# A decoder block's down projection in seven block products, ordered together with the up projection

## The chip, the cores and the metric

The kernel computes one layer of a decoder block on one core of a Trainium2 chip. The metric is the device time of one execution in microseconds (us). TensorE (PE) multiplies, VectorE (DVE), ScalarE (ACT) and GpSimd (POOL) do the rest, and SyncE (SP) issues the transfers between HBM and the core's SBUF; matmul results stand in PSUM, of which the kernel uses banks of 128x512 f32. All numbers are of type f32 outside; a change of about 0.2% is what a measurement of this kernel tells from no change.

## The reference, cut to what matters

Sequence and model width are both 1024, the inner width of the feed-forward part is 2816 = 22 x 128.

```python
mixed = (jax.nn.sigmoid(gate_a) * (o_a @ w_branch_gdn[i])
         + jax.nn.sigmoid(gate_b) * (o_b @ w_branch_nsa[i]))
h = layer_norm(DN_ALPHA * x + mixed @ w_out[i], ln1_g[i], ln1_b[i])
u = causal_dwconv(h @ w_up[i], ffn_conv_w[i])
u_g, u_v = jnp.split(u, 2, axis=-1)
f = (jax.nn.silu(u_g) * u_v) @ w_down[i]
x = layer_norm(DN_ALPHA * h + f, ln2_g[i], ln2_b[i])
```

o_a is a gated delta rule, o_b a sparse attention with compressed, selected and windowed keys. The change concerns `@ w_down`: a 1024 x 2816 gated product, stored by columns of 128 inner units, times a 2816 x 1024 weight.

## The kernel before, in words

**Precision.** An f32 operand is split into a high part (type fp32r) and a low part (what the rounding left), and each product is made of three matmuls: high by high, high by low, low by high. `mm` (L190, matmul at L191) issues each. A split is an ACT copy (high) and a subtraction (low).

**Stages.** x is transposed and v projected; then the delta rule and the input projections; then key compression; from about 630 to 895 us of the span the attention; then the branch products, W_out and the first layer norm; from about 1127 to 1499 us the up projection; from there to 1750.5 us the down projection; then what is left of the second layer norm.

**Attention.** 16 units, one for each block t of 128 tokens and group g of heads. For a unit PE makes scores for two branches (b = 0, selected keys, and b = 1, window), woven with the products by V of the unit before (`weave`, L980). The probabilities P are scaled by `scale` (L865): three of four heads by POOL (L873), one by ACT. After that PE transposes them by identity matmuls (L946), ACT copies the high part (L948) and DVE subtracts the low part (L949). L938 is POOL's scaling for the compressed keys, L882 the reciprocals' gate factors on DVE. At the end of a unit `fin` uses one buffer of the weight stream (tag `w`, three buffers, one of which holds the masks during the attention). In this stage only the order on PE is written out; the other engines' orders follow from priorities of the tile framework.

**Up projection.** 22 groups f of 128 + 128 output units (gate and value). Each group is a 2x2 block product over token halves and halves of the model width that is made in seven products of 24 or 12 matmuls in place of eight. Its sums go through DVE (`u1`, `u2`, `u3`, `c12`, `c21`, `c22`; L1480 to L1501); ACT and DVE apply the three taps of the convolution (L1382, L1466), ACT the tanh (L1508), and DVE the gating (L1512, L1513), after which the two PSUM banks a and d are free. The gated product of group f, 128 x 1024, lies in `accs` and is stored to `gdr[f]` in HBM (L1515). High weights are split by ACT, low ones by POOL (L1371) in the steady part. All this is ordered by `Plan` (L53): a list scheduler on planned durations, with pools of tokens for buffers (`ring`, `raw`, `bank`, `u`, `acc`) and due times; each engine's list is then issued in the order found.

**Down projection.** Two passes, one per token half; each goes over 22 blocks f. Per block the 512 KB of weight are loaded (`w`), split by ACT (L1564) and POOL (L1565), and the 256 KB half of `gdr[f]` (`tb`), split by ACT (L1572) and DVE (L1573); then 4 token blocks x 2 output halves x 3 matmuls of 128x512. The last KL = 6 blocks of a pass go row block by row block, so that the layer norm of one row block lies under the matmuls of the next: L1607 adds the residual, L1177 to L1187 make mean and scale (`rsqrt` on POOL, L387), L1190 normalises on ACT, L1620 and L1621 apply gain and bias.

Of the kernel before, what the change touches and what calls it, by code (L numbers as in the profile page):

```python
# [22 lines left out]
NFF = 2816 // 128  # L23
MS = {mybir.EngineType.PE}
# [28 lines left out]
class Plan:  # L53
# [16 lines left out]
    def rank(self):  # L70
# [7 lines left out]
        for n in self.nodes:  # L78
            n.late = n.asap if n.seq else (n.due if n.due is not None else n.asap + 6.0)
            n.open = n.seq or n.due is not None  # L80
# [7 lines left out]
    def run(self):  # L88
# [10 lines left out]
        while left:  # L99
# [4 lines left out]
            for e in free:  # L104
                if free[e] > t + 1e-9:
                    continue
                for n in todo[e]:
# [14 lines left out]
                    for p, tokens in n.grow:  # L122
                        back += [(n.end, p, x) for x in tokens]
# [21 lines left out]
def hybrid_block_kernel(ctx: ExitStack, tc: tile.TileContext, x, w_in, gdn_conv_w, gdn_a_log,  # L145
# [274 lines left out]
    gA = S6.tile([128, 4, T], F32, name="gA", tag="s")  # L420
    sig = [dram.tile([128, T], F32, name=f"sig{j}") for j in range(16)]
# [568 lines left out]

    prev = None
# [136 lines left out]
    gdr = [dram.tile([128, T], F32, name=f"gdr{f}") for f in range(NFF)]  # L1128
# [71 lines left out]
    P.pool("acc", 0)  # L1200
# [133 lines left out]
    def wide(_):  # L1334
# [7 lines left out]
          [stored[t] for t in range(4, 8)] + [turned[t] for t in range(4, 8)], lat=0, grow=[("acc", [0, 1])])  # L1342
# [15 lines left out]
    def make(f, n, src, deps, give=()):  # L1358

        fast = {"G": 1.25, "V": .65} if f < 3 else "G"  # L1360
# [33 lines left out]

    class Group:
        def __init__(self, f):
            self.f, self.n, self.t = f, {}, {}

        def weights(self, part):
            f = self.f  # L1400
            if part == 0:
# [5 lines left out]
                if 0 < f < AHEAD:  # L1407
                    last.give.append((w1, "raw"))
                return
            w1 = load_raw(f * 128, 0) if 0 < f < AHEAD else self.w1  # L1410
            w2 = load_raw((NFF + f) * 128, 0)
            A11, A12 = (lambda: w1.tile[:, HS[0]]), (lambda: w1.tile[:, HS[1]])
            A21, A22 = (lambda: w2.tile[:, HS[0]]), (lambda: w2.tile[:, HS[1]])
            e = {"G": 1.25, "V": .65} if f < 2 else "G"
# [8 lines left out]
            wait = [state[tt]["end"] for tt in range(4, 8)] if f == 0 else []  # L1423
# [29 lines left out]
        def after(self, n):  # L1453
# [3 lines left out]
            acc = lambda i: accs()[:, (f % 2) * 2 + i, :]  # L1457
# [31 lines left out]
            elif n == 4:  # L1489

                N["sa"] = scaled(0, "a", 0, f, [N[2], chain.get("acc", None)], take=["acc"])
# [8 lines left out]
            else:  # L1500
# [6 lines left out]
                for h, bank in enumerate("ad"):  # L1507
# [3 lines left out]
                    def g_(_, h=h, bank=bank):  # L1511
# [3 lines left out]
                N["end"] = P.add("S", 1.5, lambda _: nc.sync.dma_start(gdr[f], acc(0)), out, lat=2.0,  # L1515
                                 give=[(N["sa"], "acc")])
                chain["acc"] = N["sa"]

    groups = [Group(f) for f in range(NFF)]
# [10 lines left out]
    for f, g in enumerate(groups):  # L1530
        for n in ([6, 7, 5, 4, 3] if f < AHEAD else [1, 6, 7, 5, 2, 4, 3]):
            g.run(n)
    order = P.run()
# [7 lines left out]

    hR, l2 = [], []

    def load_rest():
        for th in range(2):
            t = S2a.tile([128, 4, D], F32, name=f"hr{th}", tag="s")
            for i in range(4):
                nc.sync.dma_start(t[:, i, :], hres[th * 4 + i])
            hR.append(t)
        for src in (ln2_g, ln2_b):  # L1550
            for hs in HS:
                t = tile_u()
                nc.sync.dma_start(t, bass.AP(tensor=src.tensor, offset=src.offset + hs.start, ap=[[0, 128], [1, 512]]))
                l2.append(t)

    wd = {}

    def down_load(th, f):
        if f % 2 == 0:
            wd["pair"] = S6.tile([128, 2, 2, D], F32R, name="wd", tag="s")  # L1560
        w = wtile()
        nc.sync.dma_start(w, w_down[f * 128:(f + 1) * 128, :])
        o = wd["pair"][:, f % 2]
        A.activation(o[:, 0], w, AF.Copy)  # L1564
        G.tensor_tensor(o[:, 1], w, o[:, 0].bitcast(F32), op=OP.subtract)  # L1565
        r = tp.tile([128, 512], F32, name="tb", tag="tb")
# [91 lines left out]
```

## Time and profile before

| | |
|---|---|
| median of 3 runs | 1762.13 us (1759.58 to 1763.2) |
| profiled execution | 1762.67 us, of which the span of the instructions is 1761.0 us |
| mean granted TensorE clock | 0.991 of full speed |
| matmuls, attention to the end of up (630 to 895, 1127 to 1499 us) | 1580 and 1622 records |
| down projection | 1056 matmuls |
| DMA over the span | 152.38 MB, 87 GB/s |

A window's row gives its stretch, its length, then for each engine the busy time with the number of records, then the granted clock, the DMA engines' share and the GB/s that they moved. A timeline's row gives start, duration, engine, line, operation, output <- inputs, shape, and in brackets the idle time before it with what ended it. A source's row gives the shortest, median and longest duration in ns. Some records of matmuls can be missing from a trace.

### The profile page before, as it was taken

The numbers are of one execution on the slowest core, as the hardware profiler recorded it, in microseconds if no ns is written. First come the engines' busy times: TensorE is split into PE (matmuls) and PEld (weight loads), VectorE is DVE, ScalarE is ACT, GpSimd is POOL, SyncE is SP. The second block draws the span as 40 slices with busy tenths as digits, with TensorE's granted clock in tenths as the row PEclk, the third lists the DMA queues.
The fourth block names the chain that finished last, engine by engine and source line by source line (L and its number), as shares of the span: only waits on it lengthen the run. The fifth ranks groups of instructions, "written<-read, shape, count | busy, mean of one in ns | idle before, by whom it ended". The sixth has DMA issues, their size and how long they took to land.

```text
span 1761.0 us, 23301 instructions
## 1 busy us (share of the span) xinstructions
PE 1719.1 (98%) x8710; PEld 1440.8 (82%) x8710; DVE 1100.4 (62%) x2068; ACT 732.2 (42%) x1282; POOL 804.8 (46%) x589
## 2 busy tenths in 40 slices
PE   8999999999999999999989999999999999999997
PEld 8888888888888877888768787788888888888886
DVE  3566757667633378899843348976666566844535
ACT  3422323233223468888732225444444444432321
POOL 1332221222213424444466236777777775764631
PEclk9999999999999999999989999999999999999999
DMA  5222121222212200000045512322222222863421
GB/s 173 73 64 72 55 74 43 74 51 61 78 62 73 68 1 1 1 1 1 25 132 191 192 48 96 108 84 84 88 80 74 89 89 96 315 223 110 171 89 48
DMA packets 157807, 152.38 MB, mean 87 GB/s; under 512 B 16329, under 2 KB 129150, under 8 KB 157694
## 3 DMA queue, kind: packets, MB, share of 16 engines
q1 hardware_dynamic: 157693, 150.89, 27.1%
q8 instruction: 69, 1.13, 0.3%
q14 instruction: 45, 0.36, 0.1%
HBM read 119.67 MB, written 31.20 MB: 86 GB/s over the span
## 4 chain that ended last, share of the span: by engine, by line
PE 85%; DVE 6%; issue 3%; ACT 2%; POOL 2%; DMA 1%; DVEq 0%; POOLq 0%; ACTq 0%; SPq 0%
PE pq L191 35%; PE big L191 33%; PE sm L191 13%; PE sm L946 3%; ACT P L911 1%; DVE st L909 1%; DVE wb L1371 1%; DVE accs L1382 0%; DVE wl L949 0%; POOL h L1228 0%; POOL h L1229 0%; DMA w<-in_w_out_dram 0%; PE big L245 0%; DVE gs L1573 0%; DVE oAl L1013 0%
## 5 line engine op out<-in xcount | busy, mean ns | idle before, releaser
L181 POOL TENSOR_TENSOR wl<-w,wh 128x1024 fp32r<-128x1024 f32 (+2 forms) x51 | 122.6, 2408 | 361.8 <-PE big L191 131.2
L191 PE MATMUL big<-xTl,wh 128*128 128x512 f32 x624 | 250.6, 402 | 0.0
L191 PE MATMUL big<-xTh,wh 128*128 128x512 f32 x624 | 250.3, 401 | 0.0
L191 PE MATMUL pq<-wd,gs 128*128 128x512 f32 x1056 | 241.5, 391 | 0.4 <-DVE accs L1513 0.4
L191 PEld LDWEIGHTS pq<-wd,gs 128*128 128x128 f32 x1056 | 198.2, 188 | 43.3 <-DVE accs L1513 0.8
L191 PE MATMUL pq<-xb,wb 128*128 128x512 f32 x792 | 189.0, 393 | 2.6 <-DVE accs L1382 2.1
L1382 DVE SCALAR_TENSOR_TENSOR accs<-pq,fcw,accs 128x510 f32<-128x510 f32 (+3 forms) x264 | 145.8, 569 | 63.3 <-ACT accs L1466 58.1
L191 PEld LDWEIGHTS pq<-xb,wb 128*128 128x128 f32 x792 | 149.7, 189 | 35.6 <-ACT wb L1172 2.5
L191 PE MATMUL big<-xTh,wl 128*128 128x512 f32 x624 | 164.1, 399 | 0.0
L873 POOL TENSOR_TENSOR P<-P,st 128x640 f32<-128x640 f32 (+7 forms) x96 | 99.8, 1067 | 127.0 <-DVE st L882 61.4
L1565 POOL TENSOR_TENSOR wd<-w,wd 128x1024 fp32r<-128x1024 f32 x44 | 112.5, 2575 | 65.3 <-ACT wd L1564 59.8
L191 PEld LDWEIGHTS big<-xTl,wh 128*128 128x128 f32 x624 | 117.7, 189 | 21.3 <-issue 0.2
L191 PEld LDWEIGHTS big<-xTh,wh 128*128 128x128 f32 x624 | 117.7, 189 | 21.1
L191 PEld LDWEIGHTS big<-xTh,wl 128*128 128x128 f32 x624 | 114.0, 188 | 22.0
L191 PE MATMUL pq<-mTh,wb 128*128 128x512 f32 x528 | 127.3, 397 | 3.2 <-ACT mTh L1172 3.1
L191 PE MATMUL pq<-mTl,wb 128*128 128x512 f32 x528 | 127.4, 391 | 0.0
L191 PEld LDWEIGHTS pq<-mTh,wb 128*128 128x128 f32 x528 | 100.8, 191 | 25.7 <-ACT mTh L1172 3.3
L1371 POOL TENSOR_TENSOR wb<-w,wb 128x512 fp32r<-128x512 f32 x79 | 102.8, 1302 | 37.8 <-ACT wb L1172 37.8
L191 PEld LDWEIGHTS pq<-mTl,wb 128*128 128x128 f32 x528 | 99.1, 188 | 21.2
L1573 DVE TENSOR_TENSOR gs<-tb,gs 128x512 fp32r<-128x512 f32 x44 | 71.4, 1641 | 67.0 <-ACT gs L1572 64.2
L949 DVE TENSOR_TENSOR wl<-sm,wh 128x512 fp32r<-128x512 f32 (+1 forms) x148 | 99.8, 684 | 13.7 <-ACT wh L948 11.3
L180 ACT ACTIVATE wh<-w 128x1024 fp32r<-128x1024 f32 (+2 forms) x51 | 53.1, 1046 | 127.1 <-PE big L191 85.9
(365 smaller groups left out, 3543.2 us busy)
## 6 DMA issues: line engine op xcount, KB each, us to landing
w<-in_w_down_dram SPq DMA_DIRECT2D x44, 512.0 KB, 4.1
w<-in_w_in_dram SPq DMA_DIRECT2D x40, 512.0 KB, 4.1
w<-in_w_up_dram SPq DMA_DIRECT2D x36, 512.0 KB, 3.8
gdr<-accs SPq DMA_DIRECT2D x22, 512.0 KB, 2.6
tb<-gdr SPq DMA_DIRECT2D x44, 256.0 KB, 3.2
sig<-th SPq DMA_DIRECT2D x32, 256.0 KB, 2.4
w<-sig SPq DMA_DIRECT2D x16, 512.0 KB, 3.4
wx<-in_w_up_dram SPq DMA_DIRECT2D x11, 512.0 KB, 3.8
```

What stands on the lines that cost most here:

```text
L180: A.activation(wh[:, :n], w[:, :n], AF.Copy)
L181: G.tensor_tensor(wl[:, :n], w[:, :n], wh[:, :n].bitcast(F32), op=OP.subtract)
L191: PE.matmul(o, a, b, start=start, stop=stop, skip_group_check=True)
L873: G.tensor_tensor(p, p, r.to_broadcast([128, p.shape[1]]), op=OP.mult)
L909: V.reduce_max(nm, pv if m > 1 else pv[:, 0], axis=AX.X, negate=True)
L911: A.activation(P[:, r0 + i, :n], pv[:, i], AF.Exp, bias=nm[:, i:i + 1], accum_out=su[:, i:i + 1])
L946: PE.transpose(tp[:n, r * 128:(r + 1) * 128], P[:, r, c0:c0 + n], ident)
L949: V.tensor_tensor(pl, tp[:n], ph.bitcast(F32), op=OP.subtract)
L1371: e.tensor_tensor(H.tile[:, 1], src(), H.tile[:, 0].bitcast(F32), op=OP.subtract)
L1382: V.scalar_tensor_tensor(o, i, fcw[:, 2 - s, j:j + 1], o, op0=OP.mult, op1=OP.add)
L1565: G.tensor_tensor(o[:, 1], w, o[:, 0].bitcast(F32), op=OP.subtract)
L1573: V.tensor_tensor(g[:, 1], r, g[:, 0].bitcast(F32), op=OP.subtract)
```

## The change

**Products.** The down projection becomes one 2x2 block product: token halves x halves of the inner width (11 blocks k each) x output halves. It is made in seven block products, in the order 1, 6, 2, 7, 5, 4, 3; each takes 11 blocks k, 4 token blocks and 3 matmuls of 128x512. Four products use a sum of gated blocks, four a sum of weight blocks.

**Sums of weights.** `down_sums` loads a piece of the four weight blocks (2 loads of 256 KB into a `w` buffer), makes four subtractions of 128x256 on POOL in the next call, and stores the sums to `wsum` in HBM (2 stores). Over 26 calls among the attention's units (one each, two where t > 2) there are 22 pieces: 88 subtractions, 44 loads, 44 stores.

**Sums of the gated product.** The up groups come in the order 0, 11, 1, 12, ... (`FORD`), so that the two groups of one k follow each other; `pair` makes four sums of 128x512 in `accs`, on DVE or POOL as the plan has it, and five stores in place of two. `acc` becomes two pools, and the buffers of a pair come free later.

**Operands.** Each product and k loads 256 KB of gated product or sum and 256 KB of weight or sum into one 128x1024 tile, split by one ACT copy and one DVE subtraction. POOL's L1565 goes. All of this, the sums of the products through a buffer `du`, and the second layer norm are now in the same `Plan` as the up stage; a due time may be given relative to the earliest start.

**Second layer norm.** Half rows are added and measured as their products end. The last product (3) ends row block by row block over its last 7 blocks k.

```diff
+    def down_sums():
+
+        if held:
+            b, k, cs = held.pop()
+            for o, x, y in ((0, 1, 0), (1, 3, 1), (3, 3, 0), (2, 2, 3)):
+                G.tensor_tensor(b[:, o], b[:, x], b[:, y], op=OP.subtract)
...
+        if summed:
+            k, c = divmod(summed.pop(0), 2)
+            cs = slice(c * 256, c * 256 + 256)
+            b = wtile().rearrange("p (b c) -> p b c", b=4)
...
             s = stats(t, g)
+            down_sums()
             weave(score_steps(s, 0), pv_steps(prev, 0) if prev else [])
             cmp_scores(s)
+            if t > 2:
+                down_sums()
             weave(score_steps(s, 1), pv_steps(prev, 1) if prev else [])
...
+    FORD = [k + KD * i for k in range(KD) for i in range(2)]
...
+        s1 = comb((1, 0), (0, 1), (2, 1), OP.add, a.out + c.out)
+        s2 = comb((1, 1), (1, 0), (0, 0), OP.subtract, [s1])
+        s3 = comb((0, 1), (0, 0), (0, 1), OP.subtract, [s1])
+        s4 = comb((3, 0), (2, 0), (1, 1), OP.subtract, [s2])
+        da = store("A", 0, HS[0], a.out)
+        dc = store("C", 2, slice(0, T), c.out)
+        db, ds, d4 = store("B", 0, HS[1], [s3]), store("S", 1, slice(0, T), [s2]), store("4", 3, HS[0], [s4])
...
+    for i in range(10):
+        P.add("X", 0, lambda _: None, [chain["make"]], take=["ring"], lat=0, grow=[("raw", None)], due=1e4)
+    SRC = {1: ("A", 0, None, 0, 0), 6: ("S", 1, 1, 0, 1), 2: ("C", 0, None, 1, 0), 7: ("B", 0, 0, 0, 1),
+           5: ("S", 0, 0, 0, 0), 4: ("C", 1, 1, 0, 0), 3: ("4", 0, None, 1, 1)}
...
+            nc.sync.dma_start(t[:, :512], gdr[b, k][:, HS[ah]])
+            src = w_down[(k + KD * up) * 128:(k + KD * up + 1) * 128, :] if r is None else wsum[r][k]
+            nc.sync.dma_start(t[:, 512:], src[:, HS[wh_]])
...
+            A.activation(DN[n, "t", k // 2][:, k % 2, 0], L.tile, AF.Copy)
...
+            V.tensor_tensor(o[:, 1], L.tile, o[:, 0].bitcast(F32), op=OP.subtract)
+        return P.add("V", 1.22, low, [Hn], give=[(L, "raw")])
...
+        mm(o, x[:, 0, ts], x[:, 0, 512:], start, False)
+        mm(o, x[:, 0, ts], x[:, 1, 512:], False, False)
+        mm(o, x[:, 1, ts], x[:, 0, 512:], False, stop)
...
+    down(7, u2)
+    u3 = [vop(.62, lambda _, t=t: V.tensor_tensor(blk(1, t), dbank["b"][t], blk(0, t), op=OP.add), [DN[7], u2[t]],
+              [(DN[7, "head"], "bank")]) for t in range(4)]
...
+    for t, e in enumerate(down(3, c22, 7)):
+        x = addrow(t, 1, bank("d", t), False, [e, pre[t, 1]], [(DN[5, "head"], "bank")])
+        finish_row(t, [half_stats(t, 1, [x]), top[t]])
...
-        G.tensor_tensor(o[:, 1], w, o[:, 0].bitcast(F32), op=OP.subtract)
...
-        V.tensor_tensor(g[:, 1], r, g[:, 0].bitcast(F32), op=OP.subtract)
```

**What moves, first pair: POOL in the attention's middle units.** P0 and P1 are the probabilities of the two halves of a unit, Pc those of the compressed keys, `w` a piece of weights. Before:

```order
L873 TENSOR_TENSOR P1_6240<-P1_6240,st_6121 128x640 x3
L873 TENSOR_TENSOR P0_6328<-P0_6328,st_6327 128x640 x3
L938 TENSOR_TENSOR Pc_6449<-Pc_6449,st_6327 128x256
L873 TENSOR_TENSOR P1_6457<-P1_6457,st_6327 128x640 x3
L873 TENSOR_TENSOR P0_6556<-P0_6556,st_6555 128x768 x3
```

With the change, in the same place:

```order
L999 TENSOR_TENSOR w_6578<-w_6578 128x256
L876 TENSOR_TENSOR P0_6443<-P0_6443,st_6433 128x640 x3
L999 TENSOR_TENSOR w_6686<-w_6686 128x256
L941 TENSOR_TENSOR Pc_6564<-Pc_6564,st_6433 128x256
L999 TENSOR_TENSOR w_6686<-w_6686 128x256
L876 TENSOR_TENSOR P1_6581<-P1_6581,st_6433 128x640 x3
L999 TENSOR_TENSOR w_6824<-w_6824 128x256 x4
L999 TENSOR_TENSOR w_6932<-w_6932 128x256 x4
L876 TENSOR_TENSOR P0_6689<-P0_6689,st_6679 128x768 x3
```

Eight subtractions now stand between the scale of one unit's P1 and that of the next unit's P0. The orders on PE, DVE and ACT through the attention are unchanged.

**Second pair: DVE at the end of a group in the up stage.** pq are PSUM banks, `accs` the gated product, `u` the sums of products. Before (gating of one group, then the sums of the next):

```order
L1512 SCALAR_TENSOR_TENSOR pq_12321<-pq_12321,accs_9918 128x512
L1513 TENSOR_TENSOR accs_9918<-pq_12321,accs_9918 128x512
L1512 SCALAR_TENSOR_TENSOR pq_12391<-pq_12391,accs_9918 128x512
L1513 TENSOR_TENSOR accs_9918<-pq_12391,accs_9918 128x512
L1480 TENSOR_TENSOR u_12537<-pq_12495,u_12508 128x512
L1483 TENSOR_TENSOR u_12555<-pq_12521,u_12537 128x512
L1485 TENSOR_TENSOR pq_12521<-pq_12542,u_12555 128x512
```

With the change, at the end of a pair:

```order
L1541 SCALAR_TENSOR_TENSOR pq_12781<-pq_12781,accs_10171 128x512
L1542 TENSOR_TENSOR accs_10171<-pq_12781,accs_10171 128x512
L1541 SCALAR_TENSOR_TENSOR pq_12851<-pq_12851,accs_10171 128x512
L1542 TENSOR_TENSOR accs_10171<-pq_12851,accs_10171 128x512
L1509 TENSOR_TENSOR u_12997<-pq_12955,u_12968 128x512
L1556 TENSOR_TENSOR accs_10171<-accs_10171 128x512 x3
L1512 TENSOR_TENSOR u_13022<-pq_12981,u_12997 128x512
L1514 TENSOR_TENSOR pq_12981<-pq_13004,u_13022 128x512
```

Three of the pair's four sums (L1556) stand behind the gating and ahead of the next group's second and third sum; the fourth is on POOL here.

**Third pair: DVE at the end of the program.** hr is the residual with the down projection added. Before, the last row block:

```order
L1607 SCALAR_TENSOR_TENSOR hr1_13419<-hr1_13419,pq_14157 128x512
L1607 SCALAR_TENSOR_TENSOR hr1_13419<-hr1_13419,pq_14158 128x512
L1177 BN_STATS bs_14825<-hr1_13419 128x6 x2
L1179 BN_AGGR ag_14828<-bs_14825 128x2
L1180 TENSOR_SCALAR ag_14828<-ag_14828 128x1
L1187 SCALAR_TENSOR_TENSOR ag_14828<-ag_14828 128x1
L1620 TENSOR_TENSOR pq_14833<-pq_14833,u_13424 128x512
L1620 TENSOR_TENSOR pq_14834<-pq_14834,u_13426 128x512
L1621 TENSOR_TENSOR hr1_13419<-pq_14833,u_13428 128x512
L1621 TENSOR_TENSOR hr1_13419<-pq_14834,u_13430 128x512
```

With the change:

```order
L1698 TENSOR_TENSOR hr0_13545<-hr0_13545,pq_14432 128x512
L1705 BN_STATS sb_13525<-hr0_13545 128x6
L1723 TENSOR_TENSOR hr0_13545<-pq_15055,u_14296 128x512
L1723 TENSOR_TENSOR hr0_13545<-pq_15058,u_14312 128x512
L1710 BN_AGGR sb_13525<-sb_13525 128x2
L1711 TENSOR_SCALAR sb_13525<-sb_13525 128x1
L1714 SCALAR_TENSOR_TENSOR sb_13525<-sb_13525 128x1
L1723 TENSOR_TENSOR hr0_13545<-pq_15071,u_14296 128x512
L1723 TENSOR_TENSOR hr0_13545<-pq_15073,u_14312 128x512
L1725 TENSOR_TENSOR hr0_13545<-hr0_13545,u_14351 128x512
```

One half is added and measured behind the last matmul; the first two L1723 belong to the row block before. One of the last two additions (L1725) is on DVE, the other on POOL.

More of the change, by code (lines that the diff above doesn't have):

```diff
@@ L1422, in s2 @@
                 node.eng.tensor_tensor(node.tile, self.s1.tile, A11(), op=OP.subtract)
-            wait = [state[tt]["end"] for tt in range(4, 8)] if f == 0 else []
+            wait = [state[tt]["end"] for tt in range(4, 8)] if self.i == 0 else []
             self.s1 = P.add(e, 1.25, s1, [w1, w2, chain["sum"]], take=["sum"], node=True)
@@ new lines, in hybrid_block_kernel, with blk, hrest, load_h @@
+    l2 = []
+    DN, dbank = {}, {}
+    def blk(i, t):
+        return state["du"][:, i, t, :]
+    def hrest(t):
+        return state["hr", t // 4][:, t % 4, :]
+    def load_h(t):
+        def f(_):
+            if t % 4 == 0:
+                state["hr", t // 4] = S2a.tile([128, 4, D], F32, name=f"hr{t // 4}", tag="s")
+            nc.sync.dma_start(hrest(t), hres[t])
+        return P.add("S", 1.8, f, [final.n[4]] if t < 4 else [final.n["end"], groups[-2].n["free"]], lat=2.0)
+    def load_l2(src, hs):
+        def f(_):
+            t = tile_u()
+            nc.sync.dma_start(t, bass.AP(tensor=src.tensor, offset=src.offset + hs.start, ap=[[0, 128], [1, 512]]))
+            l2.append(t)
+        return P.add("S", 1.0, f, [final.n["end"]], take=["u"], lat=2.0)
@@ new lines, in down_mm, with down, g_ @@
+    def down_mm(n, t, k, start, stop):
+        x = DN[n, "t", k // 2][:, k % 2]
+        o = dbank[DBANK[n]][t]
+        ts = slice(t * 128, t * 128 + 128)
+        mm(o, x[:, 0, ts], x[:, 0, 512:], start, False)
+        mm(o, x[:, 0, ts], x[:, 1, 512:], False, False)
+        mm(o, x[:, 1, ts], x[:, 0, 512:], False, stop)
+    def down(n, gate=(), late=0):
+        ends = []
+        head, tail = n in (1, 6, 7, 5, 4), n in (2, 6, 7, 4, 3)
+        prev = DN.get("pe") or chain["prod"]
+        ready = [operands(n, k) for k in range(KD)]
+        for k in range(KD - late):
+            def g_(_, k=k):
+                if head and k == 0:
+                    dbank[DBANK[n]] = [pq() for _ in range(4)]
+                for t in range(4):
+                    down_mm(n, t, k, head and k == 0, tail and k == KD - 1)
+            x = P.add("PE", 2.724, g_, [prev, ready[k]] + (list(gate) if k == 0 else []),
+                      take=["bank"] * 4 if head and k == 0 else [],
+                      give=[(DN[n, "slot", k // 2], "slot")] if k % 2 or k == KD - 1 else [], seq=True)
+            if k == 0:
+                DN[n, "head"] = x
+            prev = x
+        if late:
+            for t in range(4):
+                def g_(_, t=t):
+                    for k in range(KD - late, KD):
+                        down_mm(n, t, k, False, tail and k == KD - 1)
+                prev = P.add("PE", .681 * late, g_, [prev] + ready[KD - late:], seq=True)
+                ends.append(prev)
+        DN["pe"] = DN[n] = prev
+        return ends
@@ new lines, in hybrid_block_kernel @@
+    bank = lambda b, t: (lambda: dbank[b][t])
+    hl = [load_h(t) for t in range(NT)]
+    down(1)
+    c1 = [P.add("A", .5, lambda _, t=t: copy(blk(0, t), dbank["a"][t]), [DN[1], kept]) for t in range(4)]
+    down(6)
+    u2 = [vop(.62, lambda _, t=t: V.tensor_tensor(blk(0, t), dbank["b"][t], blk(0, t), op=OP.add), [DN[6], c1[t]],
+              [(DN[6, "head"], "bank")]) for t in range(4)]
+    down(2, c1)
+    top = [half_stats(t, 0, [addrow(t, 0, bank("a", t), True, [DN[2], hl[t]], [(DN[1, "head"], "bank")])]) for t in range(4)]
@@ L1540, in hybrid_block_kernel @@
                 n.emit()
[L1542 to L1554, printed above, removed]
```

199 lines of the change are left out of this document (115 added, 84 removed).

## The prediction

> **What bounds the kernel now.** I read the page first: the busy shares, the slices of TensorE and of its granted clock, the chain that ended last, and the group of the down projection's matmuls.
>
> ```profile
> span 1761.0 us, 23301 instructions
> PE 1719.1 (98%) x8710; PEld 1440.8 (82%) x8710; DVE 1100.4 (62%) x2068; ACT 732.2 (42%) x1282; POOL 804.8 (46%) x589
> ...
> PE   8999999999999999999989999999999999999997
> ...
> PE 85%; DVE 6%; issue 3%; ACT 2%; POOL 2%; DMA 1%; DVEq 0%; POOLq 0%; ACTq 0%; SPq 0%
> ...
> L191 PE MATMUL pq<-wd,gs 128*128 128x512 f32 x1056 | 241.5, 391 | 0.4 <-DVE accs L1513 0.4
> ```
>
> TensorE is busy 98% of the span, and the chain lies on it for 85%. The reader should see the last row: 1056 down projection matmuls take 241.5 us together, and the engine stood idle 0.4 us before them. So the stage lasts as long as its matmuls.
>
> An average can hide a stage with another limit, so next come the windows of the three stages that the change touches (columns: length, busy us of PE, of its weight loads, of DVE, ACT and POOL, granted clock, DMA share, GB/s).
>
> ```profile
> 700.00:860.00 160.00, 158.75 (x1029) 136.36 (x1028) 144.64 (x263) 134.65 (x269) 72.55 (x59) 1.00 0.01 3
> 1200.00:1480.00 280.00, 280.00 (x1230) 230.66 (x1229) 183.18 (x313) 124.19 (x206) 204.23 (x160) 1.00 0.26 83
> 1510.00:1745.00 235.00, 235.00 (x1032) 193.51 (x1031) 110.72 (x115) 68.82 (x85) 114.71 (x55) 1.00 0.46 161
> 1500.00:1600.00 100.00, 99.65 (x437) 81.75 (x436) 53.23 (x47) 40.56 (x52) 60.88 (x25) 1.00 0.72 254
> ```
>
> In the attention (first row) PE is busy 158.75 of 160 us, with DVE at 90% close behind, POOL at 45% and the DMA at 1%. In the up stage (second row) PE has no gap; DVE has 65%, POOL 73%. In the down stage (third row) PE has no gap either: 235 us for 1032 records, 0.2277 us a matmul, at a clock of 1.00. All else is under half. Work added to POOL, DVE, ACT or the DMA costs only where it makes PE late; matmuls taken away pay in full as long as nothing else rises to PE's place.
>
> **Removed: 132 matmuls.** The loops of before issue 22 x 8 x 2 x 3 = 1056; those of the change 7 products x 11 x 4 x 3 = 924, with stationary and moving operands of the same size. At 241.5/1056 = 0.2287 us each: 132 x 0.2287 = **-30.2 us**. By the steady 0.2277 it is -30.1. The stage should take 924 x 0.2287 = 211.3 us of PE.
>
> **The tail.** The chain from the last matmul on:
>
> ```profile
> 1734.78 15.75 PE pq L191 x69
> ...
> 1750.56 1.37 DVE hr L1607 x2
> 1751.93 1.21 DVE bs L1177 x2
> ...
> 1755.30 0.70 DVE pq L1620
> 1756.00 0.70 DVE pq L1620
> 1756.70 0.59 DVE hr L1621
> ```
>
> Before, two halves of the last row block are added and two measured behind the last matmul. Now one half of each was done earlier, so that one L1607 (1.37/2 = 0.68) and one L1177 (1.21/2 = 0.60) leave. One of the two last additions (0.59) goes to POOL beside DVE's, of which I count 0.4. But the order of the change (third pair of lists) puts the two multiplications of the row block before, 2 x 0.70 = 1.40, between the last block's measuring and its BN_AGGR, which DVE takes in order: by the time they are ready the last block is under way, and its chain waits behind them. -0.68 - 0.60 - 0.4 + 1.4 = **-0.3 us**; bounds -1.7 (they find a gap) and +1.4 (no gain but they).
>
> **Attention: 88 subtractions on POOL, 44 loads and 44 stores.** Nothing of this runs there now. The nearest row of the same shape is L938; beside it stand POOL's timeline over two units, one late unit, and the transposes in which PE reads what POOL scales.
>
> ```profile
> L938 POOL TENSOR_TENSOR Pc<-Pc,st 128x256 f32<-128x256 f32 x15 | 9.2, 613 | 34.0 <-ACT wh L948 16.0 <-DVE st L882 13.2 <-DVE st L881 4.8
> ```
> ```profile
> 688.55 3.04 POOL L873 TENSOR_TENSOR P<-P,st 128x512 f32<-128x512 f32 x3 [2.17 <-ACT wh L948]
> ...
> 704.94 3.68 POOL L873 TENSOR_TENSOR P<-P,st 128x640 f32<-128x640 f32 x3 [5.18 <-DVE st L931]
> 709.03 0.61 POOL L938 TENSOR_TENSOR Pc<-Pc,st 128x256 f32<-128x256 f32 x1 [0.41 <-DVE st L882]
> 714.61 3.68 POOL L873 TENSOR_TENSOR P<-P,st 128x640 f32<-128x640 f32 x3 [4.96 <-DVE st L882]
> 722.23 3.68 POOL L873 TENSOR_TENSOR P<-P,st 128x640 f32<-128x640 f32 x3 [3.94 <-DVE st L931]
> ...
> 819.44 5.60 POOL L873 TENSOR_TENSOR P<-P,st 128x1024 f32<-128x1024 f32 x3 [7.86 <-PE sm L191]
> ```
> ```profile
> 828.75 0.60 PE L946 MATMUL sm<-ident,P 128*128 128x128 f32 x4
> ```
>
> A piece is four subtractions of 128x256: 4 x 0.613 = 2.45 us. Units with t > 2 take two pieces, 4.9 us, and the order of the change puts most of them between the scale of the second half and that of the next unit's first (first pair of lists in the section on the change). Queued behind them on POOL is that scale, and PE's transposes of P wait for it. The idle time of POOL in front of it is 2.17 us at 688.55, 5.18 at 704.94, 3.94 at 722.23 and 7.86 at 819.44: in the late units it holds 4.9 us, in the middle ones about, at t = 3 not. Behind it lies more cover: at 819.44 the scale ends at 825.04 and PE reads it at 828.75, 3.7 us later. Where the idle time is missing by 1 to 2.7 us, this covers it. Bounds: 0, and 8 half units that each come 2.45 us late, +20. I take **+1**, near the low end, because the slack is seen in the rows. The 88 subtractions together are 54 us of a POOL that stands idle 55% here. The DMAs (256 KB each) go into queues at 1% use; the slot of a piece was idle, and the next piece's load is issued a half unit ahead of its subtractions. If the cover were gone, a piece would cost its 2.45 us.
>
> **Up stage: 44 combinations of 128x512 and 55 stores in place of 22.** By the compiled order 32 combinations are on DVE and 12 on POOL. Prices and the slack behind them:
>
> ```profile
> L1513 DVE TENSOR_TENSOR accs<-pq,accs x44: 679/692/693, 1129.2 to 1527.0; 128x512 f32<-128x512 f32 x44
> ```
> ```profile
> L1573 DVE TENSOR_TENSOR gs<-tb,gs x44: 671/1428/2902, 1487.8 to 1697.2; 128x512 fp32r<-128x512 f32 x44
> ```
> ```profile
> 1305.51 0.69 DVE L1513 TENSOR_TENSOR accs<-pq,accs 128x512 f32<-128x512 f32 x1
> ...
> 1318.01 2.22 PE L191 MATMUL pq<-mTh,wb 128*128 128x512 f32 x9
> ```
> ```profile
> L1371 POOL TENSOR_TENSOR wb<-w,wb 128x512 fp32r<-128x512 f32 x79 | 102.8, 1302 | 37.8 <-ACT wb L1172 37.8
> ```
>
> A combination reads two operands from SBUF, as L1573 does, which takes 0.67 us at best and 2.90 at worst with POOL at work beside it; L1513, with one operand in PSUM, holds 0.68 to 0.69 beside the same POOL. So 32 cost between 22 and 93 us of DVE time over 372 us of stage, and the share of 65% becomes 71 to 90%. I take 1.3 us each, the duration of POOL's own piece here: 42 us, 77%. The 12 on POOL add 12 x 1.3 = 16 us to its 73%: 77%. What waits behind is the release of banks: the last of a group is free at 1306.2 and the next group's first product begins at 1318.01, 12 us later; a pair's three combinations, which the order puts behind the bank release and ahead of the next sums (second pair of lists), delay those by 2 to 9 us. Bounds 0 and +15; I take **+0.5**, since the slack holds even the long case and only the first groups and the junction are tight. Stores: two more per pair of 38 us at 0.32 us of issue on SP, as `1506.61` below shows.
>
> [...]
>
> **Down stage: what feeds the products.** Per product and k there are two loads of 256 KB, one ACT copy and one DVE subtraction of 128x1024; POOL's share (112 us) goes.
>
> ```profile
> L1564 ACT ACTIVATE wd<-w 128x1024 fp32r<-128x1024 f32 x44 | 45.8, 1055 | 53.7 <-DMA w<-in_w_down_dram 47.4 <-PE pq L191 6.3
> ```
> ```profile
> L1042 DVE TENSOR_TENSOR w<-big,w x17: 692/1225/1226, 894.5 to 981.2; 128x1024 f32<-128x1024 f32 x15, 128x512 f32<-128x512 f32 x2
> ```
> ```profile
> L1045 DVE TENSOR_TENSOR w<-w x9: 691/1227/2191, 910.1 to 982.0; 128x1024 f32<-128x1024 f32 x7, 128x512 f32<-128x512 f32 x2
> ```
> ```profile
> w<-in_w_down_dram SPq DMA_DIRECT2D x44, 512.0 KB, 4.1
> ...
> tb<-gdr SPq DMA_DIRECT2D x44, 256.0 KB, 3.2
> ```
> ```profile
> 1506.61 0.32 SPq L1515 DMA_DIRECT2D gdr<-accs  x1
> ```
>
> PE takes 12 x 0.2277 = 2.73 us for one k. Beside it ACT needs 1.06; DVE 1.23; SP two issues of 0.32. In sum, against 211 us: ACT 77 x 1.06 = 81 plus some 15 for copies and norms, 45%; DVE 77 x 1.23 = 95, and from the compiled order 69 half-width operations at 0.69 with some 24 tiny ones, about 54, together 149, 70%. The loads are 77 x 0.5 = 40 MB where they were 44 x 0.77 = 35; with residual and output 0.5/2.73 us and a tenth more is about 215 GB/s, and the fourth window carried 254 for 100 us without a gap in PE. The chain of one k is a landing (4.1), ACT and DVE, 6.5 us, while ten slots let it start several k ahead. Sums of products wait on DVE, but each has a whole other product (11 x 2.73 = 30 us) before a bank or block is wanted. At the start all up products now come first (before, 20 down matmuls stood ahead of the last two); ten of the first product's eleven k are stored long before, and the eleventh is wanted 27 us in. I put junction and stage at **0**; bounds 0 and +20 (one missed k, 2.73 us, at each of seven product heads). Gone cover would cost DVE's excess over 211.
>
> **Sum.** 1762.67 (profiled execution; its span and 1.67 around it) - 30.2 - 0.3 + 1.0 + 0.5 + 0 = 1733.7. The median shown, 1762.13, is 0.5 lower than the profiled execution, so 1733.1 us, forecast as 1733.0.
>
> **Rivals.** (1) *Late scales.* The two pieces hold up P and PE waits in half the units. For it: idle time of 2.17 at 688.55, less than 4.9. Against: 3.7 us of slack behind and 7.86 in the late units. 4 to 8 late scales at 2.45 us: 10 to 20 more, 1743 to 1753. (2) *DVE late in the up stage.* All 32 take 2.9 us: DVE at 90%, banks late in perhaps half the 11 pairs by 1 to 2.5 us, 5 to 14 more: 1738 to 1747. Against: 12 us of bank slack. (3) *Slower: DVE bounds the down stage.* The 77 subtractions read two SBUF operands. If each took x, the stage lasts 77x + 54 where that exceeds 211, so from x = 2.04; slower than before by 0.2% (33 more) from x = 2.47. At L1573's longest, 2.9, it is 277 us: 1799. For it: L1045's longest is 2.19 (223 us, 1745). Against: the long ones stand beside POOL work, and POOL's 112 us of this stage are removed. (4) *The gain isn't delivered.* The heads of products wait for operands: +20, 1753. Against: PE waited 0.4 us in all for this stage's operands, with more engines in the chain.
>
> **How the numbers follow.** Main case 0.80, its own range 1730 to 1739; rival 1 0.08, rival 2 0.05, rival 3 0.03, rival 4 0.04. The low end takes the low bounds of all terms (tail -1.7, attention and up stage 0: 1762.1 - 30.2 - 1.7 = 1730.2) and 1.2 us of measurement: 1729. The high end, 1745, takes rival 2 in and the lower part of 1 and 4. About 0.2%, 3.5 us, can be told from no change: faster beyond that 0.95, within it 0.02 (rivals 1 and 4 together), slower 0.03 (rival 3).
>
> **What would show it.** Right: the down group reads x924 with about 211 us and under 1 us of idle before it; the window of the attention keeps PE within 1 us per 160; the up stage shows no wait of PE for L1541 or L1542. Wrong, by rival: idle of PE before the transposes of P; waits of PE for DVE's bank releases, combinations near 2.9 us; the subtractions of L1650 above 2 us; waits of PE at product heads for DMA landings.

## The result, and the profile after

The changed kernel takes 1730.45 us in the median of four runs (1729.77 to 1731.17), beside 1760.99 us for the kernel before on the same chip (1759.58 to 1763.2). The ratio is 0.9826, with a 95% interval of 0.9809 to 0.9843: 30.5 us less. The forecast was 1733.0 us, with a range of 1729 to 1745. A second set of runs on another occasion gave 1729.82 us (ratio 0.9825, 0.9812 to 0.9839).

The page of the changed kernel, lines as in the prediction's first fence:

```profile
span 1729.5 us, 23653 instructions
PE 1684.3 (97%) x8578; PEld 1412.4 (82%) x8578; DVE 1153.4 (67%) x2148; ACT 743.6 (43%) x1280; POOL 783.1 (45%) x650
...
L192 PE MATMUL pq<-wd 128*128 128x512 f32 x924 | 209.6, 389 | 0.0
```

The down projection's matmuls went from 1056 in 241.5 us to 924 in 209.6, and PE waited 0.0 us for their operands. PE is still the engine that sets the time.

The windows of the three stages in the changed kernel (columns as before; the down stage is shorter, so its window is too):

```profile
700.00:860.00 160.00, 157.48 (x1019) 134.55 (x1018) 146.99 (x262) 133.84 (x266) 111.77 (x114) 1.00 0.27 88
...
1200.00:1480.00 280.00, 280.00 (x1230) 230.65 (x1229) 203.05 (x334) 124.47 (x205) 216.66 (x167) 1.00 0.31 102
...
1510.00:1715.00 205.00, 205.00 (x906) 169.78 (x905) 132.22 (x165) 80.84 (x87) 20.38 (x19) 1.00 0.62 213
1500.00:1600.00 100.00, 100.00 (x442) 82.80 (x441) 64.75 (x72) 42.81 (x47) 4.03 (x2) 1.00 0.82 283
```

In the attention PE lost 1.3 us of 160 while POOL went from 45% to 70%; the prediction had "within 1 us per 160" as a sign of being right, and this one came out just beyond it. In the up stage PE has no gap with DVE at 73% and POOL at 77%. In the down stage DVE is at 64%, ACT at 39%, POOL at 10%, and the transfers run at 213 GB/s without a gap in PE, 283 in the busiest 100 us.

The end, by the chain of waits:

```profile
1717.64 0.69 DVE hr L1698
...
1718.35 0.69 DVE sb L1705
1719.05 0.60 DVE hr L1723
1719.65 0.07 issue
1719.71 2.48 POOL hr L1725 x2
1722.20 0.52 POOL sb L388
...
1722.93 0.79 ACT pq L1719
...
1725.17 1.16 DVE hr L1725
```

The last matmuls of the kernel before and of the changed kernel, by PE's timeline:

```profile
1739.63 11.57 PE L191 MATMUL pq<-wd,gs 128*128 128x512 f32 x50
```
```profile
1702.70 14.89 PE L192 MATMUL pq<-wd 128*128 128x512 f32 x65
```

In the changed kernel PE's last matmul ends at 1717.59 and the span at 1729.5: 11.9 us. In the kernel before PE ends at 1751.2 and the span at 1761.0: 9.8 us. The 1750.53 at which the chain in the prediction leaves PE is the end of the last row block's first half; three more matmuls, of its second half, run under DVE's first addition. The chain above shows what came in: the last row block's rsqrt (L388) stands on POOL behind two additions of the row block before (2.48 us).

And a place that the prediction did not speak of. Windows of the kernel before, of the kernel before in a second profile, and of the changed kernel, near 1127 us:

```profile
1123.00:1138.00 15.00, 12.90 (x50) 10.20 (x49) 12.70 (x22) 6.43 (x11) 13.31 (x11) 0.89 0.35 106
```
```profile
1123.00:1138.00 15.00, 12.97 (x50) 10.56 (x51) 12.78 (x25) 6.88 (x12) 13.50 (x11) 0.89 0.45 134
```
```profile
1123.00:1138.00 15.00, 13.49 (x60) 10.84 (x59) 12.64 (x24) 6.28 (x10) 14.84 (x12) 1.00 0.29 88
```

The granted clock is 0.89 in both profiles before and 1.00 after, in the same stretch of the program, the start of the up projection's steady part. A finer window of the first profile shows half the clock for a short time:

```profile
1129.00:1131.50 2.50, 2.50 (x8) 1.93 (x7) 2.43 (x5) 0.49 (x1) 2.33 (x2) 0.50 0.54 130
```

### The profile page after: what moved, and what is told of

It is laid out like the page before. It is cut to its first block, busy times and chain, and to the rows that moved or that the text cites. A ratio compares the mean times of both kernels' runs of the same rounds, so it can differ in the third digit from the quotient of the medians.

```text
span 1729.5 us, 23653 instructions
## 1 busy us (share of the span) xinstructions
PE 1684.3 (97%) x8578; PEld 1412.4 (82%) x8578; DVE 1153.4 (67%) x2148; ACT 743.6 (43%) x1280; POOL 783.1 (45%) x650
## 4 chain that ended last, share of the span: by engine, by line
PE 84%; DVE 7%; issue 3%; ACT 3%; POOL 2%; DMA 1%; SPq 0%; ACTq 0%; POOLq 0%; DVEq 0%
PE pq L192 34%; PE big L192 33%; PE sm L192 13%; PE sm L949 3%; DVE st L912 1%; ACT P L914 1%; DVE wl L952 1%; DVE wb L1396 0%; POOL h L1253 0%; POOL hr L1725 0%; POOL h L1254 0%; DMA w<-in_w_out_dram 0%; DVE accs L1407 0%; DMA w<-in_w_in_dram 0%; ACT wh L951 0%
## 5 line engine op out<-in xcount | busy, mean ns | idle before, releaser
L192 PE MATMUL pq<-wd 128*128 128x512 f32 x924 | 209.6, 389 | 0.0
L192 PEld LDWEIGHTS pq<-wd 128*128 128x128 f32 x924 | 173.5, 188 | 36.0
L1407 DVE SCALAR_TENSOR_TENSOR accs<-pq,fcw,accs 128x511 f32<-128x511 f32 (+3 forms) x264 | 144.3, 568 | 61.0 <-ACT accs L1495 56.1
L952 DVE TENSOR_TENSOR wl<-sm,wh 128x512 fp32r<-128x512 f32 (+1 forms) x148 | 99.4, 682 | 10.3 <-ACT wh L951 8.0
L951 ACT ACTIVATE wh<-sm 128x512 fp32r<-128x512 f32 (+1 forms) x148 | 87.1, 595 | 22.7 <-PE sm L949 19.1
L914 ACT ACTIVATE P<-big,st 128x640 f32<-128x640 f32 (+7 forms) x128 | 88.8, 701 | 10.3 <-DVE st L912 9.6
```

Source lines behind the costliest of these rows:

```text
L192: PE.matmul(o, a, b, start=start, stop=stop, skip_group_check=True)
L914: A.activation(P[:, r0 + i, :n], pv[:, i], AF.Exp, bias=nm[:, i:i + 1], accum_out=su[:, i:i + 1])
L951: A.activation(ph, tp[:n], AF.Copy)
L952: V.tensor_tensor(pl, tp[:n], ph.bitcast(F32), op=OP.subtract)
L1407: V.scalar_tensor_tensor(o, i, fcw[:, 2 - s, j:j + 1], o, op0=OP.mult, op1=OP.add)
```

## The experiments

All are the changed kernel with one edit, but for two that repeat the changed kernel and the kernel before. Where no ratio is given the time is that of one run, which alone tells about 2 us; the trace tells more.

### Eight products' worth of matmuls

```diff
-                for t in range(4):
-                    down_mm(n, t, k, head and k == 0, tail and k == KD - 1)
+                for i in range(2 if n == 6 else 1):
+                    for t in range(4):
+                        down_mm(n, t, k, head and k == 0 and i == 0, tail and k == KD - 1 and (n != 6 or i == 1))
...
```

> The changed kernel with product 6's matmuls issued twice on the same operands (so product 6 counts double in the output): 1056 matmuls as before, everything else as in the change. My theory, that the gain is the 132 matmuls alone: 132 x 0.2268 us (209.6/924 of the changed kernel's profile) = 29.9 us more than the changed kernel's 1730.5, so about 1760.4, as much as before. Rival, that part of the gain comes from POOL's removed splits or from the new order of the stage: clearly under 1755.

Measured: 1760.53 us, 1.0007 of the kernel before (0.9997 to 1.0016). With the 132 matmuls back, the whole gain is gone.

```profile
L192 PE MATMUL pq<-wd 128*128 128x512 f32 x1056 | 239.5, 389 | 0.0
```

So the sums, the removed POOL splits and the new order together don't gain or lose anything that a time can tell; the traces show parts of about 2 us that cancel, taken up below. One of them is in this row: the same 1056 matmuls take 239.5 us here and took 241.5 in the kernel before, in both of its profiles.

The starts of the single matmuls show where the 2 us were. In the kernel before, 28 of the 44 blocks have their gated product `gs`, the stationary operand, in the buffers `wh` and `wl` (f % 5 < 3, L1568 of that kernel), the other 16 in `ws`. From start to start a matmul takes 228.9 ns in the former and 226.6 ns in the latter, in both profiles, in all blocks behind the first four. In the changed kernel and in this run PE reads both operands from `wd`, and all take 226.7. For the 28 blocks of 24 matmuls the difference is 1.5 us; the stop among the first down matmuls (0.35 us idle), with the restart behind it, is 0.6. That the price goes with the buffer is what the traces show; no run moved the buffer alone, and why it matters stays open.

### DVE's subtractions in the down stage, twice and one and a half times

```diff
-            V.tensor_tensor(o[:, 1], L.tile, o[:, 0].bitcast(F32), op=OP.subtract)
+            for _ in range(2):
+                V.tensor_tensor(o[:, 1], L.tile, o[:, 0].bitcast(F32), op=OP.subtract)
...
```

> The down stage's DVE subtraction of 128x1024 made twice, 2.44 us per block in place of 1.22. By the prediction's bound the stage lasts 77x + 54 where that exceeds PE's 211: 77 x 2.44 + 54 = 242 us, so 31 us more, about 1761. If DVE has more room than that bound says (part of the 54 lies after the stage), +15 to +25. If DVE doesn't bound at all: 1731.

Measured: 1759.92 us, 29.5 more than the changed kernel. The down group's row, and the window of the stage:

```profile
L192 PE MATMUL pq<-wd 128*128 128x512 f32 x924 | 218.9, 399 | 13.4 <-DVE accs L1542 6.7 <-DVE wd L1651 5.4 <-DVE accs L1407 1.3
```
```profile
1507.00:1740.00 233.00, 219.62 (x930) 178.16 (x929) 226.68 (x244) 81.19 (x88) 18.39 (x15) 0.96 0.54 186
```

DVE is busy 226.68 of 233 us: it is the bound now. From the first down matmul (1511.02) to the last one's end (1743.28) the stage takes 232.3 us against 209.6, 22.7 more: 13.4 as waits and 9.3 as longer matmuls (218.9 against 209.6) at a granted clock of 0.96. The spans of the two profiles differ by 28.5 us; of the rest, 2.8 us lie behind the last matmul, and 3.0 ahead of the stage, where nothing was edited. So the time agrees with the 242 us of the bound partly by luck: the stage itself ends 10 us below 77x + 54, as the middle case of the expectation has it; the first of these subtractions starts at 1496.4, ahead of the first down matmul. The second edit adds a half:

```diff
             V.tensor_tensor(o[:, 1], L.tile, o[:, 0].bitcast(F32), op=OP.subtract)
+            V.tensor_tensor(o[:, 1, :512], L.tile[:, :512], o[:, 0, :512].bitcast(F32), op=OP.subtract)
...
```

> The down stage's DVE subtraction followed by a second one of half its width, about 1.9 us per block. By the bound 77 x 1.9 + 54 = 200 us, below PE's 210: no change, 1730 to 1734. If the stage's DVE cover were already used up: +52 us x the part that isn't hidden, over 1740.

Measured: 1732.64 us, 2.2 more than the changed kernel's median, which one run hardly tells; the down group took 210.2 us with 0.5 of waits. The two runs enclose the point x = 2.04 from which the prediction let DVE decide (rival 3): at 1.9 us all but hidden, at 2.45 us in force. Where between them it lies, they don't say; by the stage's 232.3 us at 2.45 I estimate 2.15, since 232.3 - 77 x 2.45 leaves 44 in place of 54.

### No sums of weights, and all of them twice

```diff
             s = stats(t, g)
-            down_sums()
...
-            if t > 2:
-                down_sums()
...
-            src = w_down[...] if r is None else wsum[r][k]
+            src = w_down[...] if r is None else w_down[(k + KD * r) * 128:(k + KD * r + 1) * 128, :]
```

> No sums of weights in the attention: no loads, subtractions or stores there; the down stage loads a weight block where it loaded a sum (so the products with sums of weights use one block alone). Theory: the sums cost 2 us inside the attention (last score matmul at 877 us in the changed kernel, 874 before), nearly all given back at its end, where PE waits for ACT's splits of oA: 1729.5 to 1730.5, the last score back at about 875. Rival, late scales that cost the program: 1725 or less.

Measured: 1729.43 us (ratio 0.9819, 0.9802 to 0.9835), 1.0 under the changed kernel, which is not clear of the spread of the runs. The trace tells more: the score matmuls of the kernel before, of the changed kernel, and of this one (the two numbers before the forms are the first and the last start):

```profile
L191 PE MATMUL big<-kS,qS x384: 218/388/522, 627.6 to 874.1; 128*128 128x512 f32 x88, 128*128 128x128 f32 x56, 128*128 128x256 f32 x24, 128*128 128x384 f32 x24
```
```profile
L192 PE MATMUL big<-kS,qS x384: 218/388/522, 628.4 to 877.2; 128*128 128x512 f32 x88, 128*128 128x128 f32 x56, 128*128 128x256 f32 x24, 128*128 128x384 f32 x24
```
```profile
L192 PE MATMUL big<-kS,qS x384: 218/388/522, 626.8 to 873.5; 128*128 128x512 f32 x88, 128*128 128x128 f32 x56, 128*128 128x256 f32 x24, 128*128 128x384 f32 x24
```

From first to last: 246.5 us before, 248.8 with the sums, 246.7 without them. The sums cost 2.1 to 2.3 us inside the attention. The second profiles agree: 246.4 us before, 248.8 with the sums. How much of it is given back at the end of the stage isn't settled. The next matmuls with oA, which wait for ACT in both kernels, start 0.5 us later in the first profiles:

```profile
895.89 0.50 PE L191 MATMUL big<-oAh,wh 128*128 128x512 f32 x1 [2.36 <-ACT wh L1028]
```
```profile
896.35 0.50 PE L192 MATMUL big<-oAh,wh 128*128 128x512 f32 x1 [2.44 <-ACT wh L1051]
```

In the second profiles they start at 895.00 and 897.07 us, 2.1 later. From the last score to this point the same instructions take 19.2 us in one profile of the changed kernel and 20.6 in the other, so that one pair can't tell what is given back.

```diff
-            for o, x, y in ((0, 1, 0), (1, 3, 1), (3, 3, 0), (2, 2, 3)):
+            for o, x, y in ((0, 1, 0), (1, 3, 1), (3, 3, 0), (2, 2, 3)) * 2:
```

> Each piece's four subtractions made twice (the second pass changes some sums, so the output differs): 88 more of 0.74 us, 65 us more of POOL in the attention. Theory, that the first 88 lie in POOL's idle time and the slack behind the scale: a unit with t > 2 now has 11.8 us of subtractions against idle times of 2 to 8 us and about 3.7 of slack, so that 10 units come late by 1 to 5 us: 10 to 40 us more, about 1750. If POOL's scales aren't waited for at all: 1731.

Measured: 1765.52 us, 35 more. The price of a subtraction, in the changed kernel, and the scores' row with twice as many:

```profile
L999 POOL TENSOR_TENSOR w<-w x88: 725/737/749, 607.8 to 817.0; 128x256 f32<-128x256 f32 x88
```
```profile
L192 PE MATMUL big<-kS,qS x384: 218/388/774, 628.1 to 908.3; 128*128 128x512 f32 x88, 128*128 128x128 f32 x56, 128*128 128x256 f32 x24, 128*128 128x384 f32 x24
```

The first 88 cost 2 us inside the stage, the next 88 another 31 (280.2 against 248.8). So they lie on idle time that is nearly used up. The size lies in the 10 to 40 that was expected, above the 20 of the forecast. That it is the scales of P that come late, the mechanism of rival 1, fits but isn't shown: the waits of PE that grew are named for DVE's L952, the low parts of the transposed P.

```profile
PE sm L949 <- DVE wl L952: 14.2, 18, 1.4
PE sm L192 <- DVE wl L952: 5.6, 8, 1.9
```

In the changed kernel these are 2.1 and 1.3 us.

### The combinations left out, and all on DVE

```diff
-            return P.add(e, 1.25, lambda g: g.tensor_tensor(block(*o), block(*x), block(*y), op=op), deps)
+            return P.add("X", 0, lambda _: None, deps, lat=0)
```

> The 44 combinations of gated blocks in the up stage left out (the stores carry what lies there, so the output differs): 32 operations less on DVE, 12 less on POOL. Theory, that they are covered by the slack of the banks: 1729.5 to 1731. Rival, that they make banks late: 1725 or less.

Measured: 1729.67 us: no difference that one run can tell.

```diff
-        e = {"G": 1.25, "V": .65}
+        e = "V"
...
```

> All 44 combinations on DVE: 12 x 0.69 = 8 us more of DVE, 12 x 1.7 = 20 us less of POOL in the up stage. Theory: no change, 1729.5 to 1732. Rival, DVE's share there as the next bound: 1735 or more.

Measured: 1731.78 us, no difference either. But the durations differ. The combinations in the changed kernel, on DVE and on POOL, and in this one:

```profile
L1556 DVE TENSOR_TENSOR accs<-accs x32: 681/694/1790, 1145.4 to 1521.5; 128x512 f32<-128x512 f32 x32
L1556 POOL TENSOR_TENSOR accs<-accs x12: 1287/1685/2271, 1146.2 to 1523.3; 128x512 f32<-128x512 f32 x12
```
```profile
L1556 DVE TENSOR_TENSOR accs<-accs x44: 676/1736/1795, 1144.3 to 1524.9; 128x512 f32<-128x512 f32 x44
```

With all 44 on DVE the median is 1736 ns in place of 694. The timeline of one pair shows when an operation is long, first in the changed kernel (DVE, then POOL), then with all on DVE:

```profile
1209.45 3.07 DVE L1556 TENSOR_TENSOR accs<-accs 128x512 f32<-128x512 f32 x3
```
```profile
1209.35 1.29 POOL L1446 TENSOR_TENSOR sb<-wx 128x512 f32<-128x512 f32 x1
1211.99 1.69 POOL L1556 TENSOR_TENSOR accs<-accs 128x512 f32<-128x512 f32 x1 [1.35 <-DVE accs L1556]
```
```profile
1209.38 6.86 DVE L1556 TENSOR_TENSOR accs<-accs 128x512 f32<-128x512 f32 x4
```

The first of the three starts while POOL's L1446 runs and takes 1.74 us. POOL's next operation is its own sum, which waits 1.35 us for DVE's; in that time the second takes 0.69. The third starts 0.2 us ahead of POOL's sum and takes 0.69 too, and the sum takes 1.69 in place of the 1.29 that POOL has at best. With all four on DVE, POOL goes on with its splits instead, and all four are long, 1.72 us in the mean. DVE's busy time from 1200 to 1480 us goes from 203.05 to 228.91, 82%, and PE stays at 280.00 of 280. That comes near the condition of rival 2 (90%), and the slack of the banks holds it.

### The tail in another order

```diff
-            y = P.add("V", .62, g_, [z, gam[h]], give=[(z, "bank")])
+            y = P.add("V", .62, g_, [z, gam[h], wv], give=[(z, "bank")])
...
-                hrest(t)[:, hs], hrest(t)[:, hs], l2[2 + h], op=OP.add), [y, bet[h]])
+                hrest(t)[:, hs], hrest(t)[:, hs], l2[2 + h], op=OP.add), [y, bet[h], wg])
```

Here wv is the next row block's TENSOR_SCALAR and wg its rsqrt.

> Each row block's multiplications wait for the next row block's TENSOR_SCALAR on DVE, its additions for the next row block's rsqrt on POOL; the work is the same. My theory of the tail: 11.9 us from the last matmul to the end of the span, of which 2.4 us are POOL's two additions of the row block before, ahead of the last rsqrt, and DVE's two multiplications ahead of them. With them moved behind, 9 to 10 us: 1728 to 1728.5. Rival, that the last transfers set the end: 1730.5, no change.

Measured: 1729.88 us (ratio 0.9823, 0.9809 to 0.9838), no gain that the time tells. In the trace PE ends at 1719.01 and the span at 1729.4: 10.4 us, 1.5 less than 11.9, where 9 to 10 was expected. It doesn't show in the span because everything from 1127 us on started 1.4 us later in this profile (1128.82 against 1127.41). The profiles of the kernels without an edit ahead of that place spread there from 1126.06 to 1130.43, so 2 us of a span are not told by one profile.

```diff
-            y = P.add("V" if (t, h) == (3, 1) else "G", 1.25, ...
+            y = P.add("V" if t == 3 else "G", .65 if t == 3 else 1.25, ...
```

The second reordering has this, and wv is the next block's last scalar operation.

> The tail once more: each row block's multiplications now wait for the next block's last scalar (after its rsqrt), POOL's additions for that rsqrt, and the last block's two additions are both on DVE. The work is the same. From the last matmul: 0.69 + 0.69 + 0.21 + 0.15 on DVE, 0.6 rsqrt, 0.2, then 1.3 of the block before beside ACT's 0.8, 4 x 0.65 and 3.2 until the transfers have landed: 9.8 us where the changed kernel has 11.9 and the first reordering 10.4. So 2 us under the control: 1728. Rival, that the transfers of the block before now land last: no gain on the control.

The control beside it is the changed kernel itself:

> The changed kernel once more, as the control of the next: 1729 to 1731, 11.9 us from the last matmul to the end of the span.

Measured: 1730.07 us (ratio 0.9828, 0.9815 to 0.9842) against 1729.82 for the control (0.9825, 0.9812 to 0.9839): no gain. From the last matmul to the end it is 1727.8 - 1716.53 = 11.3 us, not the 9.8 expected; in the control 1728.6 - 1716.77 = 11.8. Its chain ends:

```profile
1719.07 0.16 DVE sb L1716
1719.23 2.39 DVE hr L1730 x4
1721.62 1.32 DVE hr L1732
1722.95 0.60 DVEq L1801
```

DVE's work is done sooner after PE than in the changed kernel (7.0 us against 8.7), but the end of the span follows it by 4.3 us in place of 3.2. SP issues the last store at 1724.2, 0.6 us after DVE's end, behind three other stores that begin from 1721.2 on; in the changed kernel the last one goes out at once. So most of what was won is lost in the transfers, as the rival had it; what of it is the queue and what the landing isn't settled. No version that is surely faster than the changed kernel came out.

### The gap at 1127 us

The kernel before, unchanged, a second time:

> The kernel before once more, unchanged, for its profile. At about 1127 us its first profile shows PE idle for 2.10 us and then 36 matmuls in 10.03 us at a granted clock of 0.89; the changed kernel and every other one built from it show 1.5 us and 8.4 us. If this belongs to the kernel before: again about 2.1 and 10 us, and the change gains 2 us there that the prediction didn't count. If it is chance: 1.5 and 8.4 us here, and 1759 in all.

Measured: 1760.27 us. PE's row again, here of this profile and then of the changed kernel:

```profile
1125.03 10.04 PE L191 MATMUL pq<-xb,wb 128*128 128x512 f32 x36 [2.10 <-DVE accs L1382]
```
```profile
1127.41 8.43 PE L192 MATMUL pq<-xb,wb 128*128 128x512 f32 x36 [1.51 <-DVE accs L1407]
```

So it belongs to the kernel. Ahead of the operations that end PE's wait, DVE made a low weight (128x512, two operands in SBUF) in 1.34 us before and in 0.74 now, in both profiles of each; the first ones:

```profile
1123.90 1.34 DVE L1371 TENSOR_TENSOR wb<-wx,wb 128x512 fp32r<-128x512 f32 x1
```
```profile
1123.70 0.74 DVE L1396 TENSOR_TENSOR wb<-w,wb 128x512 fp32r<-128x512 f32 x1
```

To see whether the longer gap or something else costs the clock, that operation was made twice in the changed kernel:

```diff
-            e.tensor_tensor(H.tile[:, 1], src(), H.tile[:, 0].bitcast(F32), op=OP.subtract)
+            state["lows"] = state.get("lows", 0) + (e is V)
+            for _ in range(2 if e is V and state["lows"] == 13 else 1):
+                e.tensor_tensor(H.tile[:, 1], src(), H.tile[:, 0].bitcast(F32), op=OP.subtract)
```

> The changed kernel with one weight subtraction of 128x512 on DVE, the last one ahead of the taps at about 1124 us, made twice: 0.7 us more ahead of the bank release that PE waits for at about 1127. In both profiles of the kernel before, that operation took 1.34 us where the changed kernel has one of 0.74, PE idled 2.10 us where it idles 1.50 now, and the 36 matmuls behind took 10.0 us where they take 8.4. Theory, that the longer gap costs clock: idle of 2.1 to 2.2 us, a granted clock near 0.89 from 1123 to 1138 and about 10 us for the 36 matmuls. Rival, that the clock there has another cause: 2.2 us idle and 8.4 us.

Measured: 1733.83 us. PE's row and the window:

```profile
1128.67 10.04 PE L192 MATMUL pq<-xb,wb 128*128 128x512 f32 x36 [3.23 <-DVE accs L1409]
```
```profile
1123.00:1138.00 15.00, 11.77 (x45) 9.26 (x44) 12.29 (x21) 5.63 (x9) 12.65 (x11) 0.89 0.31 88
```

The two operations took 2.46 us, so the gap grew to 3.23 us, more than planned; the clock fell to 0.89 and the 36 matmuls took 10.04 us. The same 1.6 us more come at 2.10 and at 3.23 us of idle time, and nothing at 1.5, in ten profiles.

The length of a gap alone doesn't decide this. At 895 us, ahead of the first matmul with oA, the kernel before has a gap of 2.36 us in its first profile and of 2.35 in its second; over 895 to 900 us the granted clock is 0.66 in the one and 1.00 in the other. What else decides isn't settled here.

## Why the prediction was right, by its steps

The difference of the two profiled spans is 31.5 us. By stretches between marks on PE: 1.6 for the 36 matmuls at 1127 us; 32.1 for the down stage (from its first matmul to its last one's end 247.14 us less 5.47 of up matmuls in between, against 209.60); 0.2 more in the up stage, 0.1 less ahead of 1127, and 2.1 more in the tail: -1.6 - 32.1 + 0.2 - 0.1 + 2.1 = -31.5. The second profiles of both kernels give the same within 0.1 us, -1.6, -32.2, +0.2 and +2.1, but +1.5 ahead of 1127, in all -30.0; so what the change does ahead of 1127 isn't told by one pair.

**Matmuls.** Forecast -30.2, measured -32.1. 132 at the changed kernel's own 0.2267 us are 29.9; 0.6 is the stop that PE had among the first down matmuls before; 1.5 is the 2.3 ns by which the matmuls of 28 blocks were dearer. The run with eight products' matmuls confirms the count and shows the same lower price. The prediction took one price for before and after; the changed kernel's matmuls, which read other buffers, took 0.2267 us where its price was 0.2287.

**Tail.** Forecast -0.3, measured +2.1. Three of the four terms failed. The -0.68 for an addition less isn't there to be gained: in the kernel before, that addition ran under PE's last three matmuls, which the matmul term counts already, and the prediction took the end of the first half (1750.53) for the end of PE. The step "by the time they are ready the last block is under way, and its chain waits behind them" counted DVE's two multiplications and forgot POOL's queue, where the block's two additions (2.48 us) come ahead of the last rsqrt: from PE's end to the end of the rsqrt it is 5.1 us, where it was 3.1. And the 0.4 for the last addition that went to POOL didn't come: the one left on DVE took 1.16 us beside POOL's, not the 0.68 of L1621, which has an operand in PSUM where this one has both in SBUF; from the rsqrt to the end of DVE's work it is 3.6 us in both kernels. The reordering that moves POOL's additions behind the rsqrt took 1.5 us off the 11.9.

**Attention.** Forecast +1, with the price of L938. A subtraction took 0.737 us, not 0.613 (L938 reads one full operand and a broadcast column, L999 two full ones; that this makes the difference isn't shown). The stage lost 2.3 us inside; the program without the sums was 1.0 us faster, which is within the spread of the runs. That the slack holds the sums was judged rightly, and it is nearly full: the second 88 cost 31 us.

**Up stage.** Forecast +0.5 with 1.3 us a combination. Of the 32 on DVE 13 took over 1 us, and the mean was 1.06; all 13 started while an operation of POOL ran, and the other 19, at 0.68 to 0.70 us, while POOL was between two. In the run with all 44 on DVE they took 0.68 us at best, 1.74 in the median and 1.51 in the mean, more than the 1.3 of the prediction, and it cost nothing that the time tells either. The stores are three more per pair, not the two that the prediction counts; nothing rests on it. That the order of the first groups would change a gap and with it the clock, -0.6 and -1.6 us, was not among my terms; the working asked which waits the change adds, and not which ones the new order removes.

**Down stage.** Forecast 0, DVE at 70%. DVE is at 64% of the window; a subtraction took 1.22 us. The runs with 1.5 and 2 of them show that DVE becomes the bound between 1.9 and 2.45 us; 77x + 54 overstates the stage at 2.45 by 10 us. Of rival 4, no wait of PE for an operand is left in the group's row.

Against the forecast the matmuls came out 1.9 us lower, the tail 2.4 higher, the gap that wasn't counted 2.2 lower (0.6 of idle time and 1.6 of clock), and attention and up stage 0.8 lower in the first pair of profiles. That the matmuls and the tail nearly cancel is luck. The main step, that 132 matmuls fewer are worth their own time and nothing else rises to PE's place, is what the runs show.

## What to carry to other kernels

In a stage where PE had no gaps, the matmuls removed paid in full here (132 of them; put back, they cost 30.1 us), at about the price of that stage's own row, and the work of that stage that replaced them was free as long as each other engine stayed below its own bound (DVE at 64%; all but hidden at 1.9 us a block, in force at 2.45); two runs around that bound are a way to place it, and a sum of busy times that lie partly outside the stage puts it too low. Take the end of PE, and not the point where the chain leaves it, when a sum has a term for PE and one for the tail. For work on a path at the program's end, list the queue of every engine that the chain passes through, POOL's too, not only of the one whose order was looked at. Idle time can be used up: it carried 65 us of added POOL work for 2 us, and the next 65 us cost 31.

## What the runs showed of the hardware

- A gap of PE of 2.10 us, in a stretch that is else busy, came with a granted clock of 0.89 over the 15 us around it and 1.6 us more for the 36 matmuls behind it, in two profiles of one kernel (0.50 over 2.5 us of it in the first); a gap of 3.23 us cost the same 1.6; gaps of 1.49 to 1.52 us in ten other profiles at this place cost nothing. At another place gaps of 2.36 and 2.35 us came with 0.66 and with 1.00 over the next 5 us.
- Equal matmuls of 128x512 took 228.9 ns from start to start where their stationary operand lay in one pair of buffers, and 226.6 where it lay in another, block by block in both profiles of the kernel before.
- A DVE operation on 128x512 with both operands in SBUF took 0.68 us at best and 1.74 in the median with POOL busy at 77%; in the same run DVE operations on 128x512 with one operand in PSUM kept their 0.69 us (L1542: 691 to 694 ns; in the changed kernel, with POOL at 77% too, 691 to 692). POOL's operation that started 0.2 us behind one of DVE's took 1.69 us, where POOL's shortest take 1.29.
- At the end of the program two additions of 128x512 with both operands in SBUF ran on the two engines at once: 1.27 us on POOL, 1.16 on DVE. With one operand in PSUM, in the kernel before, one took 0.68 on DVE.
